# Other shares of filling matmuls in the first attention head, and the lead that they make returned over thirteen heads

## The chip, the cores and the metric

The kernel runs on one core of a Trainium2 chip. The metric is the device time of one execution, in microseconds (us). TensorE is PE in the rows below, its weight load PEld, VectorE is DVE, ScalarE is ACT, GpSimd is POOL and SyncE is SP.

## The reference

One decoder layer over 512 tokens of width 2048: a sparse-attention mixer with 16 heads of 128 in 4 groups, then a SwiGLU feed-forward part, with an RMS norm before each, residual adds and a final norm.

```
proj = h @ w_in                         # q, and three k/v pairs of each group, and gates
s_c = q @ kcc.T + bias_c                # compressed keys (31 blocks)
s_s = q @ k_selected.T + bias           # selected blocks
s_w = q @ kw.T + bias_w                 # window
o = g0 * softmax(s_c) @ vcc + g1 * softmax(s_s) @ v_selected + g2 * softmax(s_w) @ vw
h = h + o @ w_out
h = h + (silu(a) * b) @ ffn_w_out       # a, b = split(rmsnorm(h) @ ffn_w_in)
```

With 512 tokens there are 8 selection blocks and all of them may be taken, so that the selected branch and the window branch both run over all earlier keys. All of it is in float32.

## The kernel before

**Products.** A float32 product is made of three matmuls: each operand is split into a high and a low part, and high x high, low x high and high x low are added up in PSUM (`three`, L343 to L346). For weights the split is made on the way: a raw tile of 128x1024 is loaded (`Weights.load`, L86), ACT copies its high part (`whi`, L102), and DVE subtracts for the low part (`wlo`, L103). There are three raw buffers and four pairs of split ones. A product that needs the next split weights calls `W.take`, and this call writes the splits and loads of the next weights at the same place of the program, two weights ahead. So where a weight is taken decides where `whi` stands in ACT's order, and `wlo` in DVE's. `W.queue` says on which engine's queue the raw loads are issued.

**The attention stage** (L737 to L1024, about 195 to 680 us of the span) has two strands which are written into one program, and each engine runs its part in the order written.

The first strand is the attention of the 16 heads. A head has four tiles of 128 queries, tile t having 128(t+1) keys, and they come in the order 3, 2, 1, 0. `scores` (L885 to L910) makes the scores on PE (`s`), then DVE adds the bias and finds the maximum (`cx` for the compressed keys, two `u` for the other branches, L907) and ACT takes the exponential (L909). The score tile `s` in PSUM exists once, so PE's next scores wait for DVE's reading. `finish` (L912 to L924) scales by sums and gates and transposes 32x32 blocks on DVE (L914 to L922), then stores the probabilities to DRAM on SP's queue (L924). `fetch` (L928) reads them back into `ptr`, and `turn` splits them by the high part on ACT (`pth`, L945) and the low part on DVE (`ptl`, L949): two of 128 columns, two of 256, two of 384, two of 512. `values` multiplies each with the values on PE (`o`), two steps after its `turn`. In the loop over heads (12 steps each) the scores of head h+1 are written into the steps of head h; the text calls what lies between the tile-3 scores of head h and those of head h+1 **stretch h**. In stretch h PE does the scores of head h and the values of head h-1.

The second strand is the filling: `dense()`, the projections of later heads (`qpair`, `kpair`, `vpair`, on PE `proj`), and after those parts of the output projection (`partial`). It is a stream that is cut into units of three matmuls of 512 columns (six of 256), each booked at 650. `yt`, `qh` and `ql` (L396, L369, L370) on DVE and ACT belong to its ends. Four weights make a `qpair`, 32 units.

`pump(h, step)` ends each step. It writes units until the units booked reach a goal: 20800 a head (32 units) up to at = 13, and 22500 a head behind it, with at = h + (step + 4)/12. The first head has no head before it, so its scores stand ahead of the loop, with `pump(-1, min(9 + i, 11.7))` behind each of its tiles, then `pump(0, 1)`, the scores of head 1's tile 3, and `pump(0, 3)`. The raw loads of the whole stage go to POOL's queue (L975), which also issues the bias loads of head 0 and the first two fetches.

Of the kernel before, what the change touches and what calls it, by code (L numbers as in the profile page):

```python
# [43 lines left out]
TP_GAP, HN_GAP = 40, 48  # L44
RESYNC = 14
PT_STEP = 224
SPREAD, N_WARM = UL, 17


# [166 lines left out]
def nsa_block(ctx: ExitStack, tc: tile.TileContext, x, rel_bias, mix_g, ffn_g, fin_g, w_in, w_out,  # L216
              pos_k, w1k, w2k, pos_v, w1v, w2v, f_in, f_out, onehot, out):
    nc = tc.nc
    mm, act, dve, pool = nc.tensor.matmul, nc.scalar.activation, nc.vector, nc.gpsimd
# [12 lines left out]
    W = Weights(nc, rawp, convp, specs)  # L232
# [110 lines left out]
    def three(o, ah, al, bh, bl, start, stop):  # L343
        mm(o, ah, bh, start=start, stop=False, skip_group_check=True)  # L344
        mm(o, ah, bl, start=False, stop=False, skip_group_check=True)  # L345
        mm(o, al, bh, start=False, stop=stop, skip_group_check=True)  # L346

    def ws(ps, gi, g, c0=0, c1=S, start=None, end=None, of=None):

        for u in range(2):  # L350
            cs = slice(128 * u, 128 * (u + 1))
            if end and gi == 3 and u:
                W.ahead(3)
            for k in range(4):
                kk = 4 * gi + k
                st = (kk == 0) if start is None else (start and kk == 0)
                three(ps[u][:, c0:c1], g[0][:, k, cs], g[1][:, k, cs],
                      *(x[:, kk, c0:c1] for x in of or (hn_h, hn_l)), st, kk == KC - 1)
                if end and gi == 3 and k == 3:
                    end(u)  # L360
                yield 650
# [57 lines left out]
    def q_out(ps, h0):  # L419
        def end(u):  # L420
            Q[h0 + u] = tuple(qp.tile([128, S], F32R, name=f"q{n}") for n in "hl")
            split_from(normed(ps[u], SCALE), Q[h0 + u][0], Q[h0 + u][1])

        return end


    with ExitStack() as st1:
# [4 lines left out]
        def proj_tiles(n=2):  # L432
            return [(psx if next(turns) % 4 > 1 else ps1).tile([128, 512], F32, name="proj") for _ in range(n)]
# [5 lines left out]
        with ExitStack() as st0:  # L439
# [121 lines left out]
            ps = proj_tiles()  # L561
# [97 lines left out]
        ps = proj_tiles()  # L659
# [3 lines left out]
        ps = proj_tiles()  # L663
# [7 lines left out]
        ps, hk = proj_tiles(), ps1.tile([128, 256], F32, name="mlp")  # L671
# [8 lines left out]
        ps = proj_tiles()  # L680
# [5 lines left out]
        ps, hv = proj_tiles(4), ps1.tile([128, 256], F32, name="mlp")  # L686
# [30 lines left out]
        ps = proj_tiles()  # L717
        end = q_out(ps, 0)
# [18 lines left out]
    with ExitStack() as st2:  # L737
# [5 lines left out]
        CX = [ap_.tile([128, 32], F32, name=f"cx{t}", bufs=1) for t in range(NT)]  # L743
        PT = ap_.tile([128, 4, PT_STEP * 3 + runs[3]], F32, name="ptr", bufs=1)
        d_p = [dram.tile([4, 32, 4, runs[t]], F32, name=f"d_p{t}") for t in range(NT)]
# [10 lines left out]
        def proj2():  # L756
            pool_ = (psx, ps2)[next(units) % 2]
            return [pool_.tile([128, 512], F32, name="proj") for _ in range(2)]

        def qpair(h0):  # L760
            ps = proj2()
            end = q_out(ps, h0)
            for i in range(4):
                last = ws(ps, i, W.take(), end=end)
                for n, c in enumerate(last):
                    yield c
                    if h0 == H - 2 and i and n in (2, 4, 6):
                        reload_o(3 * i + n // 2 - 4)
                    if h0 == H - 2 and i == 3 and n in (0, 3):
                        split_o(n // 3)  # L770
            done["n"] += 1
            yield None
# [30 lines left out]
        def reload_o(i):  # L803

            nc.sync.dma_start(hn_l[:, i].bitcast(F32), d_o[i // 4][i % 4])

        def split_o(k):
            h, l = (x[:, 2 * k:2 * k + 2] for x in (hn_h, hn_l))
            act(h, l.bitcast(F32), AF.Copy)  # L809
            dve.tensor_tensor(l, l.bitcast(F32), h.bitcast(F32), op=OP.subtract)  # L810
# [40 lines left out]

        def pump(h, step):
            at = h + (step + 4) / STEPS
            goal = 20800 * min(at, 13) + 22500 * max(at - 13, 0)
            while done["ns"] < goal:
                c = next(stream, "end")
                if c == "end":
                    return
                done["ns"] += c or 0
# [15 lines left out]
        def load_bias(h):  # L875
            if h < H:
                TB[h] = ap_.tile([128, S], F32, name="tb")
                (nc.sync if h else pool).dma_start(TB[h], bass.AP(tensor=d_u.tensor, offset=d_u.offset + h * UL + 127,
                                                 ap=[[H * UL - 1, 128], [1, S]]))
# [32 lines left out]
        def finish(h, t):  # L912
            r = HS[h]["sm"][:, t]
            dve.reciprocal(r, r)  # L914
            dve.tensor_mul(r, r, gates[:, t, h])
            for i, p in enumerate(HS[h].pop(t)):
                o = p
                if not i:
                    o = P[t][:, :3, runs[t] - 32:]
                    p = CX[t].unsqueeze(1).to_broadcast([128, 3, 32])  # L920
                dve.tensor_scalar(o, p, r[:, i:i + 1], None, op0=OP.mult)
            dve.transpose(P[t], P[t])  # L922
            for i in range(4):
                nc.sync.dma_start(d_p[t][:, :, i].rearrange("j a r -> a j r"), P[t][32 * i:32 * (i + 1)])  # L924

        def fetch(t, queue=nc.sync):

            queue.dma_start(PT[:, :, PT_STEP * t:PT_STEP * t + runs[t]], d_p[t].rearrange("j a i r -> (j a) i r"))  # L928

        def arrived(rows, c0, t0, step):  # L930
            v = PT[:rows, :, c0:c0 + 32]
            p, i, c = v.ap
            return bass.AP(tensor=v.tensor, offset=v.offset, ap=[p, [step, NT - t0], i, c])

        def turn(h, b, kt):
            n = S - 128 * kt
            th = ap_.tile([128, 512], F32R, name="pth", bufs=3)
            tl = ap_.tile([128, 512], F32R, name="ptl") if b >= 0 else th
            rows = 128 if b >= 0 else 96
            if b < 0:  # L940
                src = arrived(rows, 64, 0, PT_STEP + 64)
            else:
                src = arrived(rows, PT_STEP * kt + 32 * (kt + 1) * b + 32 * kt, kt, PT_STEP + 32 * b)
            th4, tl4 = (x[:rows, :n].rearrange("p (t i s) -> p t i s", i=4, s=32) for x in (th, tl))
            act(th4, src, AF.Copy)  # L945
            if b < 0:
                dve.tensor_tensor(th4[32:64], src[32:64], th4[32:64].bitcast(F32), op=OP.subtract)
            else:
                dve.tensor_tensor(tl4, src, th4.bitcast(F32), op=OP.subtract)  # L949
            HS[h]["t", b, kt] = th[:rows, :n], tl[:rows, :n]  # L950
# [21 lines left out]
                split_from(o, hn_h[:, h], hn_l[:, h])  # L972
            del HS[h]

        W.queue = pool  # L975
        load_bias(0)
        load_bias(1)
        for i in range(4):
            scores(0, 3 - i)
            if i > 1:  # L980
                fetch(5 - i, pool)
            if i:
                finish(0, 4 - i)
            pump(-1, min(9 + i, 11.7))
        finish(0, 0)
        fetch(1)
        fetch(0)
        pump(0, 1)
        scores(1, 3)
        for b in range(2):  # L990
            turn(0, b, 3)
        pump(0, 3)
        for h in range(H):
            seq = [(b, kt) for kt in (3, 2, 1, 0) for b in (0, 1)] + [(-1, 0)]
            for i in range(STEPS):
                if i == 4:
                    load_bias(h + 2)
                if i == 2 and h:
                    fetch(0)
                if i < 9 and (h or i > 1):  # L1000
                    turn(h, *seq[i])
                if i == 8 and h + 1 < H:
                    fetch(3)
                    fetch(2)
                if i == 11 and h + 1 < H:
                    fetch(1)
                if i == 0 and h:
                    finish(h, 0)
                if h + 1 < H:
                    if i == 2:  # L1010
                        drain_to(needed(h + 1))
                    if i % 3 == 2 and h + i > 2:
                        scores(h + 1, 3 - i // 3)
                    elif i % 3 == 0 and i:
                        finish(h + 1, 4 - i // 3)
                if 2 <= i < 10 or i == 11:
                    if i == 2 and h % HPG == 0:
                        drain_to(h)
                    values(h, *seq[min(i - 2, 8)])
                    if i == 11:  # L1020
                        head_out(h)
                pump(h, i)
        W.queue = nc.sync
        drain_to(100)  # L1024
    mixer.close()
# [265 lines left out]
    with tc.tile_pool(name="tmp", bufs=1) as tmp:  # L1291
# [6 lines left out]
        end = plain_out(0, pa)  # L1298
# [4 lines left out]
        for p in range(N_PLAIN):  # L1303
            if p:
                pa = [ps3.tile([128, 512], F32, name="pp") for _ in range(2)]
                end = plain_out(p, pa)
# [430 lines left out]
```

## Time and profile before

| | us |
|---|---|
| median of 3 runs | 2097.61 |
| lowest, highest | 2096.29, 2098.01 |
| the profiled execution | 2096.34 |
| its span | 2094.6 |
| around the span | 1.74 |

Granted clock of TensorE over the span: 0.998. The span runs from the first to the last instruction of the profile. An idle time in brackets behind a row is that of the engine just before this instruction, with what ended it. PE's matmuls overlap: each row of three matmuls of 512 columns starts 0.23 us behind the one before while it shows 0.39 us, so a wait that is short need not show as idle time of PE.

### The profile page before, as it was taken

The page shows a single profiled execution, that of the slowest core. Times are in us where ns is not written, and L with a number is a line of the kernel's source. Part 1 is how long each engine was busy: PE and PEld are TensorE (multiplying, and loading weights), DVE is VectorE, ACT ScalarE, POOL GpSimd, SP SyncE. Part 2 cuts the span into 40 slices and gives each one's busy share as a digit, 9 for nine tenths or more (in the row PEclk, how much of TensorE's full clock was granted, in tenths as well). Part 3 has the DMA queues.
Part 4 walks back from the last instruction along what each step waited for, and adds up shares of the span by engine and source line. Part 5 has one row for each costly group of instructions (what it writes and reads, how often), then busy time and mean ns, then how long its engine had stood idle before and what let it go on. Part 6 is the DMA issues. An engine that isn't in the chain of part 4 may idle for free.

```text
span 2094.6 us, 39078 instructions
## 1 busy us (share of the span) xinstructions
PE 2075.1 (99%) x15236; PEld 1954.1 (93%) x15236; DVE 1627.6 (78%) x2705; ACT 948.6 (45%) x1524; POOL 278.2 (13%) x404
## 2 busy tenths in 40 slices
PE   9999999999999999999999999999999999999998
PEld 7898788898989889899999999999999999999997
DVE  5565777777786457898888888888888688697767
ACT  6344554555455234434434344344343455464445
POOL 2000111111111001022222132221211100000000
PEclk9999999999999999999999999999999999999999
DMA  7555767666677658578878778788755686685667
GB/s 238 171 157 155 198 192 201 189 193 191 204 218 208 240 179 213 151 209 231 216 205 224 205 223 220 196 232 215 199 158 157 208 267 187 194 295 151 196 204 279
DMA packets 321799, 427.68 MB, mean 204 GB/s; under 512 B 40300, under 2 KB 249900, under 8 KB 320973
## 3 DMA queue, kind: packets, MB, share of 16 engines
q1 hardware_dynamic: 261020, 292.18, 43.9%
q0 software_dynamic: 59696, 131.16, 25.8%
q8 instruction: 119, 1.95, 0.4%
q10 hardware_dynamic: 896, 1.84, 0.2%
q14 instruction: 68, 0.55, 0.1%
HBM read 363.12 MB, written 130.13 MB: 235 GB/s over the span
## 4 chain that ended last, share of the span: by engine, by line
PE 67%; DVE 1%; DMA 1%; ACT 0%; issue 0%; SPq 0%; DVEq 0%; ACTq 0%
PE f L344 18%; PE f L345 18%; PE f L346 18%; PE proj L344 2%; PE proj L346 2%; PE proj L345 2%; PE pp L344 1%; PE pp L346 1%; PE pp L345 1%; PE po L346 1%; PE po L344 1%; PE po L345 1%; DMA tlo<-d_w 1%; PE pp L322 0%; DMA tlo<-in_ffn_w_out 0%
## 5 line engine op out<-in xcount | busy, mean ns | idle before, releaser
L103 DVE TENSOR_TENSOR wlo<-raw,whi 128x1024 fp32r<-128x1024 f32 (+2 forms) x223 | 247.5, 1112 | 123.6 <-ACT whi L102 123.0
L102 ACT ACTIVATE whi<-raw 128x1024 fp32r<-128x1024 f32 (+2 forms) x223 | 215.9, 970 | 218.8 <-PE f L346 57.0
L346 PE MATMUL f<-hn_h,wlo 128*128 128x256 f32 x984 | 271.6, 276 | 0.0
L344 PE MATMUL f<-hn_h,whi 128*128 128x256 f32 x984 | 271.6, 276 | 0.0
L345 PE MATMUL f<-hn_l,whi 128*128 128x256 f32 x984 | 271.6, 276 | 0.0
L1229 ACT ACTIVATE whi<-raw 128x1024 fp32r<-128x1024 f32 x123 | 126.2, 1058 | 303.0 <-DVE raw L1125 299.6
L1125 DVE TENSOR_TENSOR tlo<-tt,thi 128x1536 fp32r<-128x1536 f32 (+1 forms) x83 | 145.4, 1752 | 77.8 <-ACT thi L1234 77.3
L344 PE MATMUL proj<-hn_h,whi 128*128 128x512 f32 x504 | 199.9, 397 | 0.0
L346 PE MATMUL proj<-hn_h,wlo 128*128 128x512 f32 x504 | 196.9, 391 | 0.0
L345 PE MATMUL proj<-hn_l,whi 128*128 128x512 f32 x504 | 196.9, 391 | 0.0
L345 PEld LDWEIGHTS f<-hn_l,whi 128*128 128x128 f32 x984 | 184.7, 188 | 0.0
L344 PEld LDWEIGHTS f<-hn_h,whi 128*128 128x128 f32 x984 | 184.7, 188 | 0.0
L346 PEld LDWEIGHTS f<-hn_h,wlo 128*128 128x128 f32 x984 | 184.7, 188 | 0.0
L1234 ACT ACTIVATE thi<-tt 128x1536 fp32r<-128x1536 f32 x82 | 121.9, 1486 | 72.9 <-PE f L345 61.3
L345 PE MATMUL f<-tlo,slot 128*128 128x256 f32 (+1 forms) x546 | 151.7, 278 | 0.0
L344 PE MATMUL f<-thi,slot 128*128 128x256 f32 (+1 forms) x546 | 151.6, 278 | 0.0
L346 PE MATMUL f<-thi,slot 128*128 128x256 f32 (+1 forms) x546 | 151.6, 278 | 0.0
L346 PE MATMUL proj<-whi,hn_l 128*128 128x256 f32 (+2 forms) x496 | 146.1, 295 | 2.9 <-DVE hn_l L810 2.9
L1125 DVE TENSOR_TENSOR wlo<-raw,whi 128x1024 fp32r<-128x1024 f32 x123 | 147.0, 1223 | 1.1 <-ACT whi L1229 1.1
L344 PE MATMUL proj<-whi,hn_h 128*128 128x256 f32 (+2 forms) x496 | 146.6, 295 | 0.8 <-ACT hn_h L809 0.8
L345 PE MATMUL proj<-wlo,hn_h 128*128 128x256 f32 (+2 forms) x496 | 145.6, 294 | 0.0
L345 PE MATMUL f<-wlo,slot 128*128 128x256 f32 (+1 forms) x432 | 121.4, 281 | 0.0
(406 smaller groups left out, 6459.9 us busy)
## 6 DMA issues: line engine op xcount, KB each, us to landing
raw<-in_ffn_w_in SPq DMA_DIRECT2D x135, 512.0 KB, 5.1
d_w<-in_ffn_w_out POOLq DMA_DIRECT2D x80, 512.0 KB, 8.4
rawx<-in_ffn_w_in SPq DMA_DIRECT2D x41, 512.0 KB, 4.8
raw<-in_ffn_w_out SPq DMA_DIRECT2D x73, 256.0 KB, 3.9
tlo<-d_w SPq DMA_DIRECT2D x73, 256.0 KB, 4.3
d_a<-d_a POOLq DMA_DIRECT2D x120, 128.0 KB, 5.7
slot<-d_a SPq DMA_DIRECT2D x18, 768.0 KB, 6.7
raw<-in_nsa_w_in POOLq DMA_DIRECT2D x24, 512.0 KB, 5.0
```

What stands on the lines that cost most here:

```text
L102: self.nc.scalar.activation(hi[:, :n], src, AF.Copy)
L103: self.nc.vector.tensor_tensor(lo[:, :n], src, hi[:, :n].bitcast(F32), op=OP.subtract)
L344: mm(o, ah, bh, start=start, stop=False, skip_group_check=True)
L345: mm(o, ah, bl, start=False, stop=False, skip_group_check=True)
L346: mm(o, al, bh, start=False, stop=stop, skip_group_check=True)
L1125: dve.tensor_tensor(o, a, b, op=OP.subtract)
L1229: act(h, r, AF.Copy)
L1234: act(h, ttf, AF.Copy)
```

## The change

The goal of `pump` gets a lead: 3900 (six units) at the stage's beginning, and less by the same part for each step until it is nothing at at = 13. What the first head writes is no longer a share of this goal, but counts of units: 4, 6, 9 and 11 behind its four tiles, 15 ahead of head 1's tile-3 scores, and 22 behind the first two `turn`s; the first two steps of the loop do not pump. `W.ahead(2)` behind the last tile's scores writes the splits for two weights there, and one `take` has an ahead of one instead of two. The raw loads change to POOL's queue only behind these 22 units.

```diff
+LEAD = 3900
@@ qpair
-                last = ws(ps, i, W.take(), end=end)
+                last = ws(ps, i, W.take(1 if h0 == 2 and i == 1 else 2), end=end)
@@ pump
             at = h + (step + 4) / STEPS
-            goal = 20800 * min(at, 13) + 22500 * max(at - 13, 0)
+            pump_to(20800 * min(at, 13) + 22500 * max(at - 13, 0) + LEAD * max(1 - at / 13, 0))
+
+        def pump_to(goal):
             while done["ns"] < goal:
@@
-        W.queue = pool
         load_bias(0)
         load_bias(1)
         for i in range(4):
@@
             if i:
                 finish(0, 4 - i)
-            pump(-1, min(9 + i, 11.7))
+            if i == 3:
+                W.ahead(2)
+            pump_to(650 * (4, 6, 9, 11)[i])
         finish(0, 0)
         fetch(1)
         fetch(0)
-        pump(0, 1)
+        pump_to(650 * 15)
         scores(1, 3)
         for b in range(2):
             turn(0, b, 3)
-        pump(0, 3)
+        pump_to(650 * 22)
+        W.queue = pool
         for h in range(H):
@@
-                pump(h, i)
+                if h or i > 1:
+                    pump(h, i)
```

On PE the matmuls stay the same, and only the place of units among them changes. Between scores (S with the tile) and values (o with the key tile and the branch) there are, counted in units:

| | before | after |
|---|---|---|
| head 0 | S3 3 S2 3 S1 2 S0 6 | S3 4 S2 2 S1 3 S0 6 |
| stretch 1 | S3 5 o30 o31 o20 3 S2 ... | S3 7 o30 o31 3 o20 3 S2 ... |
| stretch 9, S3 to o01 | 18 | 18 |
| stretch 10, S3 to o01 | 18 | 19 |
| done at S3 of heads 1, 2 | 14, 46 | 15, 51 |
| done at S3 of heads 8, 9, 10 | 238, 270, 302 | 240, 272, 303 |
| done at S3 of heads 11, 12, 13 | 334, 366, 398 | 335, 367, 398 |

Here the heads in the last three lines are those whose tile-3 scores come next. From head 13's tile-3 scores on, the units stand as before.

On SP, in the first head, with d_p the stores of tiles 3, 2, 1, 0 and ptr the fetches; before:

```order
L924 DMA d_p_1880<-p_1871 32x4x160 x4
L924 DMA d_p_1879<-p_1870 32x4x96 x4
L928 DMA ptr<-d_p_1880 128x4x160
L928 DMA ptr<-d_p_1879 128x4x96
L924 DMA d_p_1882<-p_1873 32x4x288 x4
```

and after:

```order
L927 DMA d_p_1880<-p_1871 32x4x160 x4
L87 DMA raw<-in_nsa_w_in 128x4x128 x2
L927 DMA d_p_1879<-p_1870 32x4x96 x4
L931 DMA ptr<-d_p_1880 128x4x160
L931 DMA ptr<-d_p_1879 128x4x96
L87 DMA raw<-in_nsa_w_in 128x4x128 x2
L927 DMA d_p_1882<-p_1873 32x4x288 x4
```

Two raw tiles, in two pieces each, have come over from POOL.

On DVE, in stretch 9, from the last `u` of tile 3 to the tiles of 384 columns; before:

```order
L907 ISA u,mx<-s,tb 128x512
L907 ISA mx 128x1
L949 TENSOR_TENSOR ptl<-ptr,pth 128x256
L914 RECIPROCAL sm<-sm 128x3
L915 TENSOR_TENSOR sm<-sm,gates 128x3
L921 TENSOR_SCALAR p_1873<-cx_1877,sm 128x3x32
L921 TENSOR_SCALAR p_1873<-p_1873,sm 128x4x128 x2
L922 STREAM_TRANSPOSE p_1873<-p_1873 128x1152
L103 TENSOR_TENSOR wlo<-raw,whi 128x1024
L949 TENSOR_TENSOR ptl<-ptr,pth 128x384 x2
```

and after:

```order
L910 ISA u,mx<-s,tb 128x512
L910 ISA mx 128x1
L104 TENSOR_TENSOR wlo<-raw,whi 128x1024
L952 TENSOR_TENSOR ptl<-ptr,pth 128x256
L917 RECIPROCAL sm<-sm 128x3
L918 TENSOR_TENSOR sm<-sm,gates 128x3
L924 TENSOR_SCALAR p_1873<-cx_1877,sm 128x3x32
L924 TENSOR_SCALAR p_1873<-p_1873,sm 128x4x128 x2
L925 STREAM_TRANSPOSE p_1873<-p_1873 128x1152
L952 TENSOR_TENSOR ptl<-ptr,pth 128x384 x2
```

The low part of a weight has moved from behind the transposition to the place right behind the scores; on ACT `whi` has moved likewise, from behind the `pth` of 256 to right behind the exponentials. On DVE, further on in stretch 9, from the first `ptl` of 512 columns on; before:

```order
L949 TENSOR_TENSOR ptl<-ptr,pth 128x512
L914 RECIPROCAL sm<-sm 128x3
L915 TENSOR_TENSOR sm<-sm,gates 128x3
L921 TENSOR_SCALAR p_1872<-cx_1876,sm 128x3x32
L921 TENSOR_SCALAR p_1872<-p_1872,sm 128x4x96 x2
L922 STREAM_TRANSPOSE p_1872<-p_1872 128x896
L103 TENSOR_TENSOR wlo<-raw,whi 128x1024
L949 TENSOR_TENSOR ptl<-ptr,pth 128x512
L396 SCALAR_TENSOR_TENSOR yt<-proj,ybc 128x512
L370 TENSOR_TENSOR ql<-yt,qh 128x512
L103 TENSOR_TENSOR wlo<-raw,whi 128x1024
```

and after:

```order
L104 TENSOR_TENSOR wlo<-raw,whi 128x1024
L952 TENSOR_TENSOR ptl<-ptr,pth 128x512
L917 RECIPROCAL sm<-sm 128x3
L918 TENSOR_TENSOR sm<-sm,gates 128x3
L924 TENSOR_SCALAR p_1872<-cx_1876,sm 128x3x32
L924 TENSOR_SCALAR p_1872<-p_1872,sm 128x4x96 x2
L925 STREAM_TRANSPOSE p_1872<-p_1872 128x896
L397 SCALAR_TENSOR_TENSOR yt<-proj,ybc 128x512
L371 TENSOR_TENSOR ql<-yt,qh 128x512
L104 TENSOR_TENSOR wlo<-raw,whi 128x1024
L952 TENSOR_TENSOR ptl<-ptr,pth 128x512
```

Both low parts and one `yt` with its `ql` now stand ahead of the second `ptl` of 512, where one low part did.

From the tile-3 scores of a stretch to its second `ptl` of 512, DVE's order holds, more than before: in stretch 1 a low part and two pairs of `yt` and `ql`; in 2 and 3 two such pairs; in 4 two `v0l` (a value projection's end in place of `yt` and `ql`); in 5 to 7 one pair; in 8 a low part and two `v0l`; in 9 and 10 a low part and one pair; in 11 one pair; in 12 and 13 nothing. In 2 to 7 the first low part stands between the two `ptl` of 384; in 8 to 13 the first two stand right behind the scores of tiles 3 and 2, as shown. What has come ahead of the second `ptl` of 512 is missing behind it.

## Rows read from the trace of the kernel before

**Rows 1.** The page: span, and busy time of each engine over it.

```profile
span 2094.6 us, 39078 instructions
PE 2075.1 (99%) x15236; PEld 1954.1 (93%) x15236; DVE 1627.6 (78%) x2705; ACT 948.6 (45%) x1524; POOL 278.2 (13%) x404
```

**Rows 2.** Waits of PE, 195 to 580 us: total, times, longest.

```profile
PE o L344 <- ACT pth L945: 1.7, 1, 1.7
PE s L344 <- DVE mx L907: 1.6, 2, 0.9
PE o L344 <- issue: 0.6, 1, 0.6
```

**Rows 3.** Timeline of PE, head 0: start, duration, operation, idle before and releaser.

```profile
201.31 0.39 PE L344 MATMUL proj<-hn_h,whi 128*128 128x512 f32 x1
...
202.00 0.40 PE L344 MATMUL proj<-hn_h,whi 128*128 128x512 f32 x1
...
204.41 0.40 PE L344 MATMUL s<-k0h,qh 128*128 128x288 f32 x1 [0.88 <-DVE mx L907]
...
210.73 0.40 PE L344 MATMUL s<-k0h,qh 128*128 128x288 f32 x1 [0.77 <-DVE mx L907]
...
220.98 0.30 PE L344 MATMUL o<-pth,v0h 128*128 128x128 f32 x1 [0.62 <-issue]
...
223.70 0.38 PE L344 MATMUL o<-pth,v0h 128*128 128x256 f32 x1 [1.66 <-ACT pth L945]
```

**Rows 4.** DMA issues, 190 to 235 us: xcount, KB each, us to landing.

```profile
raw<-in_nsa_w_in SPq DMA_DIRECT2D x4, 256.0 KB, 3.0
raw<-in_nsa_w_in POOLq DMA_DIRECT2D x4, 256.0 KB, 4.7
```

**Rows 5.** Timeline of ACT: the first parts of 256 columns, stretch 1.

```profile
223.23 0.72 ACT L945 ACTIVATE pth<-ptr 128x256 fp32r<-128x256 f32 x2 [1.20 <-DMA ptr<-d_p]
```

**Rows 6.** A head's busy time: us, PE, PEld, DVE, ACT, POOL, clock, DMA share, GB/s.

```profile
460.00:490.00 30.00, 30.00 (x147) 24.95 (x146) 23.60 (x67) 15.12 (x40) 4.47 (x6) 1.00 0.69 192
```

**Rows 7.** Waits of DVE and ACT, 460 to 490 us: total, times, longest.

```profile
ACT cx L909 <- DVE mx L907: 10.5, 4, 3.7
DVE ptl L949 <- ACT pth L945: 4.2, 3, 1.5
...
DVE ql L370 <- ACT qh L369: 1.4, 2, 0.7
```

**Rows 8.** Timeline of DVE, stretch 9, and the next stretch's first row.

```profile
460.54 0.18 DVE L907 CUSTOM_DVE_ANT_0 cx<-s,biasc 128x31 f32<-128x31 f32 x1
...
463.24 0.43 DVE L949 TENSOR_TENSOR ptl<-ptr,pth 128x256 fp32r<-128x256 f32 x1 [1.28 <-ACT pth L945]
...
475.12 0.68 DVE L949 TENSOR_TENSOR ptl<-ptr,pth 128x512 fp32r<-128x512 f32 x1
...
477.10 0.69 DVE L370 TENSOR_TENSOR ql<-yt,qh 128x512 fp32r<-128x512 f32 x1 [0.70 <-ACT qh L369]
...
478.05 1.23 DVE L103 TENSOR_TENSOR wlo<-raw,whi 128x1024 fp32r<-128x1024 f32 x1 [0.26 <-ACT whi L102]
...
490.44 0.18 DVE L907 CUSTOM_DVE_ANT_0 cx<-s,biasc 128x31 f32<-128x31 f32 x1
```

**Rows 9.** Timeline of PE: stretch 9's first and last tile-3 scores, its o01, stretch 13's beginning.

```profile
457.16 0.29 PE L344 MATMUL s<-k0h,qh 128*128 128x288 f32 x1
...
458.46 0.28 PE L346 MATMUL s<-k0h,ql 128*128 128x256 f32 x1
...
476.23 0.39 PE L345 MATMUL o<-ptl,v0h 128*128 128x512 f32 x1
...
576.85 0.29 PE L344 MATMUL s<-k1h,qh 128*128 128x288 f32 x1
```

**Rows 10.** Timeline of DVE, stretch 14, where a low part stands right behind the scores.

```profile
617.52 0.18 DVE L907 CUSTOM_DVE_ANT_0 cx<-s,biasc 128x31 f32<-128x31 f32 x1
...
620.86 1.22 DVE L103 TENSOR_TENSOR wlo<-raw,whi 128x1024 fp32r<-128x1024 f32 x1 [1.93 <-ACT whi L102]
```

## The prediction, made before the changed kernel was timed

> **What bounds the kernel now.** I read the page first. PE is busy 2075.1 of 2094.6 us [rows 1], so a change of order can gain only some of the 19.5 us that are left, or lose by making PE wait. The change touches the attention stage alone, so next I read what PE waits for there, from the first scores to head 13: three lines, 1.7 + 1.6 + 0.6 = 3.9 us, five waits [rows 2]. The timeline puts all of that into 20 us of head 0 [rows 3]: 0.88 and 0.77 ahead of the scores of tiles 2 and 0, which wait until DVE has read the ones before them, then 0.62 and 1.66 ahead of the first values of 128 and of 256 columns. Idle time understates a wait, since matmuls overlap. From start to start, against the pitch usual for the same shape, these four stand at 1.04, 0.94, 0.78 and 1.83, and the matmuls behind the last two at 0.17 and 0.35: **5.1 us**. That is all that the first head can give.
>
> Behind head 0 the stage looks calm: PE is busy 30.00 of 30.00, DVE 23.60, ACT 15.12 [rows 6]. But I asked what DVE and ACT do in the rest of their time. DVE's waits are for ACT (`ptl` for `pth` 4.2, `ql` for `qh` 1.4), ACT's longest is for DVE (10.5) [rows 7]: in this stretch DVE waits for neither PE nor a transfer. They run as a loop of their own, and its period, from `cx` at 460.54 to `cx` at 490.44, is 29.90 [rows 8]. PE's tile-3 scores start at 457.16 in stretch 9 and at 576.85 in stretch 13 [rows 9], 29.92 a head. A head's 32 units at 0.69 (202.00 less 201.31 [rows 3]) are 22.1, and its scores and values are 7.6 by the pitch of their shapes: 29.7, so some 0.25 a head is already waits, about 1.5 us from head 7 on. The two loops go at the same pace, and the slack between them is small: DVE's second `ptl` of 512 columns starts at 475.12 and takes 0.68, so it is ready at 475.80, and PE uses it at 476.23 [rows 8, 9]. **0.43 us is what DVE may be later there.**
>
> **Part 1: head 0's shares.** By the last score tile 9 units instead of 8 are in place, and between the values of 128 and of 256 columns stand three where there was none. One unit of 0.69 comes into waits on DVE that PE would sit through: of 1.04 + 0.94, 1.3 stays. The 2 units more ahead of the first values (1.4) cover 0.78 and 0.17, and the three behind them (2.1) the 1.83 and 0.35. Gain 0.69 + 3.13 = **3.8 us**; by idle times alone 0.69 + 0.62 + 1.66 = 3.0 (low end); 5.1 is the most.
>
> **Part 2: the queue.** Four issues of 256 KB go from POOL to SP, where the same shape lands in 3.0 instead of 4.7 [rows 4]. Behind them on SP wait the stores of tile 0 and, for the second pair, head 1's first stores. The first pair runs beside the fetch on which `pth` of 256 waited 1.20 [rows 5], and takes transfer time from it. No row shows this meeting. Its cost is from 0 (ACT's wait is met by the three new units) to 1.7, the difference of the two landing times, taken as a measure of what a transfer loses to its neighbours there; no gain, as no split waits for these loads. I take 0, nearest to what the cover gives, and keep 1.7 for the range.
>
> **Part 3: the lead and its return.** Units are moved, not added. But a unit that comes earlier takes its weight earlier, and `whi` and `wlo` move up in ACT's and DVE's order past `pth` and `ptl`, which PE needs at a fixed place. I count X, from `cx` to the end of the second `ptl` of 512. Before, X = 475.80 - 460.54 = 15.26 [rows 8].
>
> In stretches 9 and 10 three things are added. A low part right behind the scores waits for its `whi`, which waits for the exponentials: 1.93 [rows 10] where `ptl` waited 1.28 [rows 8], +0.65. The same again in tile 2: +0.5. Ahead of the second `ptl` of 512 stand one more low part (1.18 at the spacing of its kind; the row with a wait shows 1.23), `yt` and `ql` (0.68 and 0.69), `ql`'s wait of 0.70 and the low part's 0.26, less what overlaps: +3.4 [rows 8]. X = 15.3 + 0.65 + 0.5 + 3.4 = 19.8, taken as 20.0.
>
> PE asks for it 476.23 - 458.74 = 17.5 after its tile-3 scores end (the last starts at 458.46 and takes 0.28 [rows 9]), with 18 units between; with 19 it is 18.2. So the wait is D + X - 17.5 or - 18.2, where D is how far `cx` starts behind the end of the scores (1.80 in stretch 9 before). PE's waits shorten D again, down to nearly 0 (I take 0.14). In stretch 9, D = 0.25 gives **2.75**; DVE's order then takes longer than PE's, D grows to 1.3, and stretch 10 gives **3.0**. Stretch 11, with one pair more (X about 18.7), gives 1.25; stretch 8, with a low part and two `v0l`, 0.5; stretch 12 has X as before, 0. Sum 7.5.
>
> Stretch 1 has the most on DVE ahead of both `ptl` of 512 (a low part, two pairs): 1.2 for the first and 2.2 for the second, 3.4. Stretches 2 and 3, with two pairs, X = 18.7 and PE 18 or 19 units behind: 0.7 and 1.35, 2.0. Stretches 4 to 6: 0, stretch 7: 0.7. Stretch 13, where PE is at its known waits and two low parts come earlier, +1.5.
>
> **Sum.** Waits before: 5.1 + 1.5 = 6.6. After, to stretch 12: 1.3 (head 0) + 3.4 + 2.0 + 0.7 + 7.5 = 14.9. With stretch 13's 1.5 that is +9.8. Nothing behind takes it back, for from head 13's scores on the units stand as before and PE is the bound. The profiled execution took 2096.34 us, 1.74 more than its span; 2096.3 + 9.8 = **2106 us**. It lies 1.3 under the median of 2097.6 and at the lowest of the three runs, so against the median the same sum would read 2107.4.
>
> The least by this reckoning is D at its floor of 0.14 everywhere: 2.65 + 1.9 + 1.0 for stretches 9 to 11, 2.5 in stretches 1 to 3, 1.3 in head 0 and nothing else, 9.4 against 6.6 with up to 1.5 for stretch 13: +3 to +5, so 2099 to 2101. The most is the sum with part 2's 1.7 and part 1's low end (+0.8): 2108.5.
>
> **A rule against this.** DVE's 23.60 and ACT's 15.12 of 30.00 [rows 6] leave room on both. The Trainium skill (Perfetto Trace Analysis, Identifying the Most-Contended Engine) calls occupancy a fair measure for Vector and Scalar and says to optimise the engine with the highest first; by it neither of the two limits anything here, and filling PE's gaps pays in full; the time that this gives is the first rival's, below. The rows of waits speak against it: two half-idle engines that wait for each other have a period of 29.90 [rows 7, 8].
>
> **The rivals.**
>
> *The loop has room, and the change pays (faster).* With `wlo` and `yt` moved, DVE works while it waited for `pth` before; up to 4.2 + 1.4 = 5.6 of a head [rows 7] could be filled, and the order of stretches 2 to 6, which puts the low part between two `ptl` of 384, shortens the loop. Then DVE comes ahead of PE by a microsecond a head, D is at its floor when stretch 9 begins, and what is late there is made up. Price: part 1's 3.8, with up to 1.5 of the small waits: 2091 to 2092.5. Against it: PE's use of the second `ptl` of 512 is at 17.5 or 18.2 whatever D is, and X stands at 20. It decides if X is below 18 in stretches 9 to 11, that is if the added 4.6 is under 2.7.
>
> *Gain and loss cancel (same).* Part 1's 3.8 comes, and the late stretches cost half of what I reckon: D at its floor, and X about 19. 3.8 + 1.5 gained against 3.4 + 2 or so: 2096 to 2101.
>
> *Slower, by the first stretch's fetch rather than the order.* The raw loads on SP keep back head 0's fetch, PE waits there up to 1.7, and the rest cancels: 2098.
>
> **How the numbers follow.** A difference of 0.2%, 4.2 us, is about what a measurement of this kernel can tell from no change, so faster is under 2093.4 and slower over 2101.8. Slower by DVE's order has 0.65, most of it from 2102 to 2109, with likeliest 2106. The two cases inside the bound have 0.24 together, 2095 to 2101.8, and the gain 0.11. The range, 2095 to 2110, takes in the first two, with 1.5 above the most for a loop whose lag grows on; what is left out is the gain and a little more loss.
>
> **What would show it.** PE's waits in head 0 on `pth` are gone, and the ones on `mx` are near 1.3: part 1. New waits of PE on `ptl` (values of 512 columns) in stretches 1 to 3 and, longest, 9 and 10, some 3 us each; DVE's period from `cx` to `cx` there at 32 to 33, not 29.9: part 3. Tile-3 scores of head 13 at 585 instead of 576.85. I am wrong if they start at or before 577, if PE waits for no `ptl` in stretches 9 to 11, or if the second `ptl` of 512 ends less than 18 us behind `cx` there; and wrong on the queue if `pth` of 256 in stretch 1 waits over 2 us for its fetch and PE with it.

## Result: slower by twice what was forecast

The changed kernel takes 2115.83 us (median of 5 runs, 2114.91 to 2117.60), the kernel before 2096.43 (5 runs): a ratio of 1.0092, interval 1.0077 to 1.0107, or 19.4 us. The forecast was 2106.0, with 2095 to 2110: right in its sign and in where the loss sits, outside its range in size. The profiled execution took 2116.36 us, with a span of 2114.6.

The page of the changed kernel, against [rows 1]: PE's busy time grew by only 7 us, the span by 20.

```profile
span 2114.6 us, 39085 instructions
PE 2082.2 (98%) x15236; PEld 1955.8 (92%) x15236; DVE 1629.6 (77%) x2705; ACT 948.4 (45%) x1524; POOL 275.4 (13%) x400
```

PE's waits from 195 to 600 us (total, times, longest), against [rows 2]. The one wait for `pth` of 1.7 has become seven, and ten for `ptl` are new:

```profile
PE o L345 <- ACT pth L948: 7.6, 7, 2.3
PE o L346 <- DVE ptl L952: 6.1, 10, 0.9
PE s L345 <- DVE mx L910: 1.2, 3, 0.5
```

That is 14.9 us of idle time where [rows 2] add up to 3.9; 0.9 of it lies in stretch 13, which begins at 593.03, so 14.0 stands ahead of it. More than half is PE's wait for ACT's `pth`. Tile-3 scores of head 13 start at 593.03 instead of 576.85 [rows 9], 16.2 later. From head 15's scores to the last 30 us of the kernel the distance stays between 18.7 and 18.8 us, so nearly all of the loss was made in the attention stage and nothing gives it back. The last 30 us add another 1.2, to the 20.0 between the two spans.

To place it, I took each matmul's distance to the next, less the usual distance for its shape, and added these up by stretch, split into those ahead of which PE idled and those that were slow without an idle time. The measured columns are differences to the kernel before, row by row; the forecast's rows for 2 to 12 are waits as they would be afterwards, with those of before taken off in a line of their own, and its other rows are differences too:

| | forecast | measured | of it waits | of it slow matmuls |
|---|---|---|---|---|
| head 0 | -0.7 | -0.7 | -1.0 | +0.3 |
| stretch 1 | +0.3 | 0.0 | +0.4 | -0.4 |
| 2 and 3 | +2.0 | +2.6 | +2.4 | +0.2 |
| 4 to 7 | +0.7 | +0.9 | +0.8 | +0.1 |
| 8 | +0.5 | +1.85 | +1.7 | +0.1 |
| 9 | +2.75 | +5.05 | +3.5 | +1.6 |
| 10 | +3.0 | +4.15 | +2.7 | +1.5 |
| 11 | +1.25 | +1.7 | +1.6 | +0.1 |
| 12 | 0.0 | +0.7 | +0.7 | +0.1 |
| waits of before in 7 to 12 | -1.5 | off in each row | | |
| 13 | +1.5 | +1.6 | +1.1 | +0.5 |
| 14 to the end | 0.0 | +2.1 | | |

Stretches 8 to 12 hold 13.5 of the 20.0 us between the two spans, where 6.0 was forecast.

DVE in stretch 9, against [rows 8]: the low parts stand where the order put them, and the first waits 1.93 for its `whi`, as in [rows 10].

```profile
465.45 0.18 DVE L910 CUSTOM_DVE_ANT_0 cx<-s,biasc 128x31 f32<-128x31 f32 x1
...
468.79 1.22 DVE L104 TENSOR_TENSOR wlo<-raw,whi 128x1024 fp32r<-128x1024 f32 x1 [1.93 <-ACT whi L103]
...
477.39 1.23 DVE L104 TENSOR_TENSOR wlo<-raw,whi 128x1024 fp32r<-128x1024 f32 x1 [1.85 <-ACT whi L103]
...
483.85 1.23 DVE L104 TENSOR_TENSOR wlo<-raw,whi 128x1024 fp32r<-128x1024 f32 x1 [0.25 <-ACT whi L103]
484.99 0.68 DVE L952 TENSOR_TENSOR ptl<-ptr,pth 128x512 fp32r<-128x512 f32 x1
```

From `cx` to the end of the second `ptl` of 512 it is 485.67 - 465.45 = 20.2 us (X, before 15.26). PE's rows there, against 476.23 in [rows 9], which had no idle time:

```profile
484.39 0.50 PE L345 MATMUL o<-pth,v0h 128*128 128x512 f32 x1 [2.26 <-ACT pth L948]
485.73 0.49 PE L346 MATMUL o<-ptl,v0h 128*128 128x512 f32 x1 [0.84 <-DVE ptl L952]
...
487.92 0.63 PE L346 MATMUL proj<-hn_l,whi 128*128 128x512 f32 x1
...
490.17 0.39 PE L346 MATMUL proj<-hn_l,whi 128*128 128x512 f32 x1
```

PE waits first for ACT's `pth`, which stands behind `qh` and `whi` on ACT, then for the `ptl` made from it. ACT itself was free: its `qh` waited 4.36 for DVE's `yt`.

```profile
482.24 0.63 ACT L370 ACTIVATE qh<-yt 128x512 fp32r<-128x512 f32 x1 [4.36 <-DVE yt L397]
482.77 1.04 ACT L103 ACTIVATE whi<-raw 128x1024 fp32r<-128x1024 f32 x1
483.72 0.61 ACT L948 ACTIVATE pth<-ptr 128x512 fp32r<-128x512 f32 x1
```

Among ACT's waits from 430 to 580 there is none of a `whi` for its raw load, so the loads, which moved with the splits, were not late. Behind PE's waits, a unit's matmuls take 0.63 instead of 0.39. The windows say why (us, busy time of PE, PEld, DVE, ACT, POOL, granted clock, DMA share, GB/s):

```profile
484.00:486.00 2.00, 0.77 (x2) 0.46 (x3) 2.00 (x3) 0.33 (x1) 0.52 (x1) 1.00 0.27 66
486.00:488.00 2.00, 2.00 (x7) 1.53 (x7) 1.27 (x3) 1.15 (x2) 0.22 (x1) 0.59 0.52 127
488.00:490.00 2.00, 2.00 (x7) 1.56 (x6) 1.26 (x7) 1.36 (x6) 0.00 (x0) 0.55 0.45 155
490.00:492.00 2.00, 2.00 (x11) 1.64 (x10) 1.79 (x6) 0.08 (x1) 0.00 (x0) 1.00 0.95 311
```

The granted clock falls to between 0.5 and 0.6 behind the two waits, that is mostly 1.2 GHz, and is back at 2.4 by 490. Such a fall is in the trace of before too, behind a wait of 2.15 us at 607.86 (stretch 13, the same columns), and I had read that place without making a price of it:

```profile
606.00:608.00 2.00, 0.14 (x1) 0.14 (x2) 2.00 (x3) 0.00 (x0) 0.00 (x0) 1.00 1.08 352
608.00:610.00 2.00, 2.00 (x10) 2.00 (x11) 1.47 (x7) 0.92 (x5) 0.00 (x0) 0.54 0.98 257
```

### The profile page after: what moved, and what is told of

The parts are those of the page before. It is cut to its first block, busy times and chain, and to the rows that moved or that the text cites. A ratio compares the mean times of both kernels' runs of the same rounds, so it can differ in the third digit from the quotient of the medians.

```text
span 2114.6 us, 39085 instructions
## 1 busy us (share of the span) xinstructions
PE 2082.2 (98%) x15236; PEld 1955.8 (92%) x15236; DVE 1629.6 (77%) x2705; ACT 948.4 (45%) x1524; POOL 275.4 (13%) x400
## 4 chain that ended last, share of the span: by engine, by line
PE 68%; DVE 1%; DMA 0%; ACT 0%; issue 0%; DVEq 0%; ACTq 0%
PE f L346 19%; PE f L345 19%; PE f L347 19%; PE proj L345 2%; PE proj L346 2%; PE proj L347 2%; PE pp L347 1%; PE pp L346 1%; PE pp L345 1%; PE po L346 1%; PE po L347 1%; PE po L345 1%; PE pp L323 0%; DMA tlo<-in_ffn_w_out 0%; DVE slot L1134 0%; PE o L346 0%
```

## The experiments

The theory after this reading: the loss is DVE's (and ACT's) order around the second `ptl` of 512, and a share of it the clock. The rivals: head 0's shares or the queue; units that stand in other places on PE; a loss that grows with the lead. Four kernels first, on one chip, where the kernel before took 2099.85 us (16 runs).

**No lead.** LEAD = 0; head 0's shares and the queue change stay.

```diff
-LEAD = 3900
+LEAD = 0
```

> The changed kernel with a lead of 0: head 0 keeps its new shares and the queue change, stretch 1 has 31 units instead of 36, and from stretch 2 on DVE's and PE's order is that of before. If the loss comes from the lead's order of DVE in the later stretches (theory), all of it goes: tile-3 scores of head 13 within 2 us of 576.85, waits of PE on ptl in stretches 2 to 12 as before, and a time of 2093 to 2097 us, since head 0 gives 0.7 to 3 us. If head 0's shares or the queue cause the loss (rival), it stays over 2105 us.

Measured: 2099.18 us (11 runs), ratio 0.9994 (0.9985 to 1.0003). Head 13's scores start at 577.60, and DVE's X is 15.3 in stretches 2 to 12 (15.6 in 10). So neither head 0's shares nor the queue costs anything that can be measured, and the whole loss hangs on the lead. The expected 2093 to 2097 were counted from 2096.4, so from 3.4 less to 0.6 more than before; measured are 0.7 less, inside the noise. The shares alone gain nothing that can be told: head 0 gives its 0.7, and then PE runs into the values of 256 columns without the three units ahead of them.

```profile
224.18 0.39 PE L345 MATMUL o<-pth,v0h 128*128 128x256 f32 x1 [2.02 <-ACT pth L948]
```

The clock is 0.67 and 0.50 in the four microseconds from 224, and stretch 1 is 0.8 us worse than before: 0.4 less in waits, 1.3 more in slow matmuls.

**Splits one step later.** What a `take` asks for is written behind the next step's `turn` and `finish` in the loop's heads 7 to 12; PE's order stays.

```diff
     def ahead(self, n):
+        self.want = max(self.want, self.nt + n)
+        if not self.hold:
+            self.flush()
+
+    def flush(self):
         last = len(self.specs)
-        while self.ncv < min(self.nt + n, last):
+        while self.ncv < min(self.want, last):
@@
+                W.flush()
+                W.hold = 7 <= h < 13
                 if h or i > 1:
                     pump(h, i)
+                W.hold = False
```

> The changed kernel, but in the loop's heads 7 to 12 the splits and loads that a take asks for are written one step later, behind the next step's turn and finish. PE's order of matmuls stays that of the changed kernel; on ACT and DVE the low parts of stretches 8 to 12 stand again where they stood before, and only one yt with its ql (or two v0l) still stands ahead of the second ptl of 512. Theory (DVE's order makes PE wait): X in stretches 9 and 10 falls from 20.2 to about 17.3, PE waits there under 1 us each, the clock stays at 1.00 there, and 9 to 11 of the 13.5 us lost in stretches 8 to 12 come back: 2103 to 2108 us. Rival (the places of the units on PE themselves cost it, or the lead as such): 2113 to 2117 us.

Measured: 2106.57 us (5 runs), ratio 1.0032 (1.0019 to 1.0045). PE's waits from 425 to 555 us, first here and then in the changed kernel (425 to 570):

```profile
PE o L351 <- DVE ptl L957: 0.9, 3, 0.3
PE s L350 <- DVE mx L915: 0.2, 1, 0.2
```

```profile
PE o L345 <- ACT pth L948: 5.3, 4, 2.3
PE o L346 <- DVE ptl L952: 2.8, 4, 0.8
```

X is 17.3 in stretches 9 and 10, no clock falls there, and 11.5 of the 13.5 us of stretches 8 to 12 are back. PE's matmuls stand exactly as in the changed kernel, so their places cost at most the 2 us that are left; the `yt` and `ql` that still stand ahead of the `ptl` can account for these, which is not shown by itself. Over the whole stage 9.6 us came back and not 11.5, because stretches 13 and 14, where the held splits end, took some 1.2 more and stretch 1 varied by 0.5.

**Raw loads on POOL again**, all else changed.

```diff
+        W.queue = pool
         load_bias(0)
@@
         pump_to(650 * 22)
-        W.queue = pool
```

> The changed kernel with only the queue undone: raw loads on POOL from before head 0, as before. Theory (the queue is worth nothing): within 1.5 us of the changed kernel's 2115.8. Rival (the raw loads on SP hold back head 0's fetch, up to 1.7 us): 2114 or less, with pth of 256 in stretch 1 waiting less than 1.0.

Measured: 2117.13 us (4 runs), ratio 1.0079 (1.0066 to 1.0093), inside the changed kernel's own interval. The queue is worth nothing that can be measured. In the changed kernel `pth` of 256 waits 1.02 for its fetch in stretch 1, not the 1.20 of [rows 5], and with the loads on POOL it waits 1.27; the feared meeting of the loads and the fetch does not show.

**Doses of DVE time** in the kernel before, to measure PE's wait and the clock by themselves.

```diff
                 dve.tensor_tensor(tl4, src, th4.bitcast(F32), op=OP.subtract)
+                if b == 1 and kt == 0:
+                    for _ in range({3: 2, 5: 4, 7: 6, 9: 8}.get(h, 0)):
+                        dve.tensor_tensor(tl4, src, th4.bitcast(F32), op=OP.subtract)
```

> The kernel before, with the last subtraction of the second ptl of 512 columns repeated 2, 4, 6 and 8 times more in stretches 4, 6, 8 and 10 (0.61 us each: 1.2, 2.4, 3.7, 4.9 us of DVE, the result is the same). Nothing else is moved. Both theories expect PE to wait 0.8, 2.0, 3.2 and 4.5 us for it, a slack of 0.43 less, 10.5 together. Theory A (a longer wait also lowers TensorE's clock, as the trace of the changed kernel shows in stretches 9 and 10): behind the two or three longer ones the granted clock falls to between 0.5 and 0.7 for some 4 us, at 1.6 us each: 2110 to 2113 us. Theory B (the slow matmuls in stretches 9 and 10 have another cause): clock 1.00 all through, 2106 to 2108 us.

Measured: 2116.12 us (4 runs), ratio 1.0073 (1.0058 to 1.0088). The expected times were counted from 2096.4; against the kernel before on the same chip it is 16.3 us more, where theory A had 14 to 17 and theory B 10 to 12. In the traces 1.3 us more stand in stretch 1, ahead of the first dose (below). PE's rows behind the four doses:

```profile
328.79 0.50 PE L345 MATMUL o<-ptl,v0h 128*128 128x512 f32 x1 [0.29 <-DVE ptl L952]
...
391.93 0.50 PE L345 MATMUL o<-ptl,v1h 128*128 128x512 f32 x1 [2.37 <-DVE ptl L952]
...
456.81 0.80 PE L345 MATMUL o<-ptl,v1h 128*128 128x512 f32 x1 [3.69 <-DVE ptl L952]
...
523.62 0.50 PE L345 MATMUL o<-ptl,v0h 128*128 128x512 f32 x1 [4.41 <-DVE ptl L952]
```

10.8 us of idle time where 10.5 was expected, but that the sums meet is partly luck: a dose took 0.73 and not 0.61 (X is 21.1 with eight of them), and D differs from stretch to stretch. With the D and X of this trace, the prediction's D + X - 17.5 gives 0.4, 2.7, 4.4 and 4.4 us, so the way from DVE's lateness to PE's wait is right. And the windows behind the second, third and fourth:

```profile
392.00:394.00 2.00, 2.00 (x9) 1.67 (x10) 1.17 (x2) 1.49 (x2) 0.00 (x0) 1.00 0.11 31
...
458.00:460.00 2.00, 2.00 (x7) 1.52 (x6) 1.51 (x3) 1.13 (x2) 0.00 (x0) 0.50 0.00 0
460.00:462.00 2.00, 2.00 (x6) 1.61 (x5) 1.47 (x7) 1.16 (x5) 1.50 (x2) 0.50 0.18 20
...
524.00:526.00 2.00, 2.00 (x7) 1.58 (x6) 1.04 (x3) 1.80 (x3) 0.00 (x0) 0.55 0.00 0
526.00:528.00 2.00, 2.00 (x7) 1.59 (x6) 1.94 (x5) 0.29 (x1) 0.56 (x1) 0.59 0.00 0
```

Nothing else had been moved, so the waits themselves bring the fall. Its price was some 3 us behind 3.69 and 1.7 behind 4.41, and nothing behind 2.37: it is not a fixed sum, and the length of a wait alone does not tell whether it comes.

That shows best in stretch 1, where this kernel is still the kernel before. The wait ahead of the values of 256 columns was 1.66 in the trace of before [rows 3], and the clock stayed up; here it was 1.53, and the clock fell. First the window of before, then row and window of this run:

```profile
224.00:226.00 2.00, 1.92 (x10) 1.58 (x10) 1.88 (x8) 0.00 (x0) 1.26 (x2) 1.00 0.61 160
```

```profile
223.70 0.48 PE L344 MATMUL o<-pth,v0h 128*128 128x256 f32 x1 [1.53 <-ACT pth L945]
...
224.00:226.00 2.00, 2.00 (x6) 1.59 (x6) 1.92 (x7) 0.00 (x0) 1.39 (x2) 0.50 0.75 177
```

In the same way the waits of 1.34 and 0.30 in stretch 1 of the changed kernel (239.83 and 240.63) left the clock at 1.00, and those of 1.35 and 0.30 in the kernel with the loads on POOL brought it to 0.52. So a fall of some 1.3 to 2 us comes and goes in stretch 1 without any change in PE's order.

**A lead that is kept: two, three, four, five units.** If the place of the takes in a step sets DVE's order, the loss should not grow with the lead, but go up and down. These four keep one lead to at = 12.9, so that PE's order in stretches 2 to 12 is that of before, to the unit, and only the phase of the takes differs.

```diff
-LEAD = 3900
+LEAD = 1300        # 1950, 2600, 3250
@@
-            pump_to(... + LEAD * max(1 - at / 13, 0))
+            pump_to(... + (LEAD if at < 12.9 else 0))
```

> The changed kernel with a lead of two units that isn't given back step by step but kept until at = 12.9. PE's order in stretches 2 to 12 is then that of before, to the unit; on DVE the order of stretches 8 to 10 of the changed kernel (a low part right behind the scores of tiles 3 and 2, and a third one with yt and ql ahead of the second ptl of 512) stands in every stretch from 2 to 12. Theory (the loss is DVE's order, set by where in a step the takes fall): each of the 11 stretches loses 3 to 4.5 us, waits and clock together, as 9 and 10 did in the changed kernel: 2128 to 2148 us. Rival (the loss grows with the lead, or comes from units standing in other places on PE): with a third of the lead and PE's order of before, 2096 to 2102 us.

> As the kernel with a lead of two units, with three. On DVE no low part stands right behind the scores; ahead of the second ptl of 512 stand one yt with its ql (or two v0l) more than before, as in stretch 7 of the changed kernel, which lost 0.86 us. Theory: X near 17.6, 0.5 to 1 us in each of 11 stretches, clock 1.00: 2101 to 2108 us. Rival (loss grows with the lead): more than with a lead of two.

> As the kernel with a lead of two units, with four. DVE's order in stretches 2 to 12 is that of stretches 5 and 6 of the changed kernel, which lost nothing. Theory: nothing is lost in stretches 2 to 12, head 0 gives 0.7 to 1, and stretch 13, where the lead ends, is unknown within 3 us: 2093 to 2099 us. Rival (loss grows with the lead): the slowest of the three.

> As the kernels with a kept lead of two, three and four units, with five. DVE's order in stretches 2 to 12 is that of stretches 2 to 4 of the changed kernel: two pairs of yt and ql ahead of the second ptl of 512 (lost 1.1 and 1.5 there), or two v0l (lost nothing). Theory: 8 stretches at 1.1 to 1.5 and 3 at about 0, less head 0's gain: 6 to 11 us more than before, clock 1.00. Rival (four units or more are enough, the loss of shorter leads being one of too little lead): as with four.

The kernel before took 2098.62 us beside the first three (15 runs) and 2098.70 beside the fourth (21 runs). X and the period from `cx` to `cx` are those of stretch 10, and D is how far `cx` starts behind the end of the scores:

| lead | time | ratio (interval) | D | X | period |
|---|---|---|---|---|---|
| none (before) | | | 1.66 | 15.3 | 29.9 |
| 2 units | 2155.95 | 1.0270 (1.0254 to 1.0285) | 0.61 | 20.1 | 34.5 |
| 3 units | 2109.41 | 1.0049 (1.0035 to 1.0063) | 0.72 | 17.8 | 31.0 |
| 4 units | 2095.58 | 0.9988 (0.9979 to 0.9996) | 0.61 | 15.9 | 29.7 |
| 5 units | 2113.54 | 1.0072 (1.0058 to 1.0086) | 0.61 | 18.4 | 31.5 |

A lead of two units costs 57 us, one of four gains: a loss that grows with the lead is out, and so are the places of the units on PE, which are the same in all four in stretches 2 to 12. The smallest lead puts the order of stretches 8 to 10 of the changed kernel into all eleven stretches, and each costs about what stretches 9 and 10 cost there. PE's waits from 195 to 640 us with two units, and with four (the second run of it, below):

```profile
PE o L345 <- ACT pth L948: 22.9, 13, 2.1
PE o L346 <- DVE ptl L952: 10.1, 12, 0.8
```

```profile
PE o L346 <- DVE ptl L952: 5.5, 5, 3.1
PE s L345 <- DVE mx L910: 0.7, 2, 0.5
PE o L345 <- ACT pth L948: 0.6, 2, 0.5
```

DVE's `cx` of stretches 9 and 10 and the second `ptl` of 512 of the latter, with two units:

```profile
499.06 0.18 DVE L910 CUSTOM_DVE_ANT_0 cx<-s,biasc 128x31 f32<-128x31 f32 x1
...
518.38 0.68 DVE L952 TENSOR_TENSOR ptl<-ptr,pth 128x512 fp32r<-128x512 f32 x1
...
533.70 0.18 DVE L910 CUSTOM_DVE_ANT_0 cx<-s,biasc 128x31 f32<-128x31 f32 x1
```

and with four:

```profile
460.61 0.19 DVE L910 CUSTOM_DVE_ANT_0 cx<-s,biasc 128x31 f32<-128x31 f32 x1
...
475.82 0.68 DVE L952 TENSOR_TENSOR ptl<-ptr,pth 128x512 fp32r<-128x512 f32 x1
...
490.22 0.18 DVE L910 CUSTOM_DVE_ANT_0 cx<-s,biasc 128x31 f32<-128x31 f32 x1
```

In these rows it is stretch 9: 518.38 + 0.68 - 499.06 = 20.0 against 475.82 + 0.68 - 460.61 = 15.9, and a period of 34.6 against 29.6. With X = 15.9 and D = 0.61 the `ptl` is ready 16.5 behind the scores, a microsecond before PE's 17.5, and the loop takes PE's own 29.7. Two units cost 57.3 us more than before where 32 to 52 was expected: the eleven stretches cost 4.9 us more than before on average, 3.1 in waits and 1.8 in slow matmuls, and stretch 1, which the expectation left out, adds 4.5. Three units cost 10.8 (5 to 12 expected), five 14.8 (6 to 11 expected): there the stretches with two pairs cost 1.3 to 1.8 each, and stretch 1 adds 1.5, with a fall of the clock in it.

**Four units again, and ended earlier** (at = 12.4 in place of 12.9).

> The kernel with a kept lead of four units once more, for its interval. Theory: head 0 and stretch 1 give 3 us, stretches 4, 8 and 12 (with two v0l ahead of the second ptl of 512) cost 1 together: 2 to 4 us less than before, a ratio of 0.9980 to 0.9992. Rival (the first comparison was chance): 0.9995 or more.

> The kernel with a kept lead of four units, with the lead taken back at at = 12.4 instead of 12.9, so that stretch 13 has DVE's order of before and not two splits of reloaded heads and a low part ahead of its second ptl of 512, for which PE waits 3.1 us in the kernel with the lead to 12.9. Theory: stretch 13 costs 7.3 as before instead of 7.9, up to 2 less if the clock doesn't fall: 0.3 to 2 us less than the kernel with the lead to 12.9. Rival (the units missing behind stretch 12's values make PE wait elsewhere): 1 to 3 us more.

Measured: 2096.20 us, ratio 0.9990 (0.9981 to 0.9998), and 2095.86, ratio 0.9987 (0.9978 to 0.9996), 11 runs each against 21 of before. Both beat before and the changed kernel; the gain of 2 to 3 us is at the edge of what can be told, but three comparisons agree, two of which share the same runs of before. In the traces, head 0 and stretch 1 together stand at 3.0 us over the pitch with four units where they stood at 5.9 before: **this is part 1's gain, 2.9 us**, against 3.0 to 3.8 as reckoned. Stretches 4, 8 and 12, with their two `v0l`, still make PE wait 0.3 to 0.7 for `ptl`, where the first expectation let nothing be lost. The two ends differ by nothing that can be measured: the earlier one trades the `ptl` wait of 3.1 in stretch 13 for the `hn_l` waits of before.

**Splits of the reloaded heads on POOL**, in the kernel before. Stretch 13 holds 7.3 us over the pitch, more than head 0, so it looked like the place to gain.

```diff
             act(h, l.bitcast(F32), AF.Copy)
-            dve.tensor_tensor(l, l.bitcast(F32), h.bitcast(F32), op=OP.subtract)
+            pool.tensor_tensor(l, l.bitcast(F32), h.bitcast(F32), op=OP.subtract)
```

> The kernel before with the six subtractions of the reloaded heads (hn_l, line 810) on POOL instead of DVE. It bears on where this stage can still gain: stretch 13 holds 7.3 us of waits and slow matmuls, more than head 0's 5.1. If DVE's load there is the cause (theory), 7.2 us less on DVE in stretches 13 and 14 brings 3 to 6 us: 2091 to 2094 us. Rival: POOL is slower than DVE at it, and PE waits for POOL instead: 2096 to 2105 us.

Measured: 2106.50 us (4 runs), ratio 1.0038 (1.0023 to 1.0052); the rival holds. POOL's operation, and PE's longest new wait (195 to 640 us):

```profile
L810 POOL TENSOR_TENSOR hn_l<-hn_l,hn_h x6: 2341/2362/2418, 599.7 to 624.2; 128x1024 fp32r<-128x1024 f32 x6
```

```profile
PE proj L346 <- POOL hn_l L810: 5.0, 4, 1.6
```

2.36 us each where DVE takes 1.2 (1.18 to 1.23 for the same six in the trace of before), and PE waits for them.

## Why the prediction was right in sign and short in size

**Part 1** holds: 0.7 in the scores as reckoned, the value waits of head 0 gone from the trace, 2.9 us where a lead follows that does no harm.

**Part 2** holds: nothing that can be measured. The 1.7 kept for the range was not needed.

**Part 3** holds in its mechanism, and X was right where it was worked out from rows: 20.0 reckoned for stretches 9 and 10, 20.2 and 20.1 measured; 18.7 for stretch 11, 18.4 measured; the waits stand ahead of the second tile of 512 columns, in the stretches that were named. One sign was drawn too narrowly: the waits were to be on `ptl`, and more than half of the idle time is on the `pth` from which it is made (2.26 of 3.10 in stretch 9), because the late `yt` on DVE holds back ACT's order too. What failed are terms of the sum:

1. **The clock had no term.** Behind the waits of stretches 9 and 10 PE ran at about half its rate for some 4 us: +3.1 us, put at nothing. The price could have been read from stretch 13 of before, where a wait of 2.15 is followed by a clock of 0.54 (above) and some 1.7 us of slow matmuls.
2. **D's floor.** I took 0.14; measured, `cx` never starts less than 0.61 behind the end that the profile shows for the scores. That alone is about 0.5 in stretches 2, 3 and 11 and 0.6 in stretch 9 (D 0.85 instead of 0.25). In stretch 10 D was to grow to 1.3 and fell back to 0.61, so the waits there were 2.7 where 3.0 was forecast: PE's wait takes the lag away again.
3. **Stretches 8 and 12.** I gave stretch 8's low part and two `v0l` a wait of 0.5, with no working shown; X was 19.7 and the loss 1.85. The `v0l` wait for their `v0h` on ACT, and the low part behind them for its `whi`:

```profile
449.10 0.44 DVE L404 SCALAR_TENSOR_TENSOR v0l<-proj,ymul,v0h 128x256 fp32r<-128x256 f32 x1
450.08 0.48 DVE L404 SCALAR_TENSOR_TENSOR v0l<-proj,ymul,v0h 128x256 fp32r<-128x256 f32 x1 [0.54 <-ACT v0h L403]
451.03 1.23 DVE L104 TENSOR_TENSOR wlo<-raw,whi 128x1024 fp32r<-128x1024 f32 x1 [0.46 <-ACT whi L103]
```

From the first `v0l` to the low part's start it is 1.93, of which 1.0 is waiting. Stretch 12 was to have X as before and lose nothing; X was 16.6, and PE waited 0.53 for DVE ahead of the tile-0 scores.

4. **The credit of 1.5** for waits already there in stretches 7 to 12 was about right and hides part of the miss. In the trace of before, the first scores of tile 0 start 0.2 to 0.3 late in stretches 7, 9, 10 and 11 without an idle time that shows, and a value in stretch 8 as much; in the changed kernel these are gone. In stretch 9 of before it is 0.38 from a unit's last matmul to the scores, where 0.23 is usual:

```profile
480.58 0.39 PE L346 MATMUL proj<-hn_h,wlo 128*128 128x512 f32 x1
480.96 0.40 PE L344 MATMUL s<-k0h,qh 128*128 128x288 f32 x1
```

The measured column has them taken off in each row, so stretches 8 to 12 stand at some 15 us of waits and slow matmuls where 7.5 was forecast.

5. **Behind stretch 13** I let nothing be lost; 2 us were. One is in stretch 14, which starts with DVE later behind PE (`cx` 4.35 behind the first scores instead of 3.34), and 1.2 in the last 30 us of the kernel, of which no run here shows the cause. Nor do all units stand as before from head 13's scores on: twice in stretch 13 there are 3 and 2 units between two values where there were 2 and 3.

The sum of idle times came out near by chance: 14.9 forecast to stretch 12, 14.0 in the view of waits. But 6.6 was taken off for before where the same view shows 3.9, and a wait costs more than its idle time. That is counted from the end shown for a matmul, 0.16 behind the point where the next one usually starts (0.39 against 0.23), the first matmul behind a wait hands on some 0.1 later, and the clock may fall.

**The rivals.** That the loop has room was to be decided by X below 18 in stretches 9 to 11; it was 18.4 to 20.2, so it fell for this change. As a mechanism it is real: with a lead of four X is 15.9 and the change pays. Occupancy, the ground for it, does not tell these cases apart: over stretches 2 to 12 DVE is busy for 261 us with two units and for 257 with four, ACT for 170 and 169, and 60 us lie between the two kernels. That gain and loss cancel needed X about 19 and stretches 9 to 11 at 2 us or so; they cost 10.9. The transfer rival fell with the queue.

What stays open: why waits of the same length, at the same place of the same order, bring the clock down in one execution and not in another, and why 2.37 us left it alone.

## To carry to other kernels

When filling work is moved, don't stop at the engine that it fills: list what each moved unit pulls along on the other engines, and count for every consumer how long the feeding engine now takes from its fixed start (here X) against the time at which it is asked for. Here the order depended on the phase and not on the amount, so try neighbouring amounts (two, three, four, five units) before judging a schedule. A wait of TensorE of 1.3 us or more, alone or with a second one right behind it, should be priced with a fall of the clock, 1.3 to 3 us here, and as a range that begins at nothing, since it does not always come.

## What the runs showed of the hardware

Waits of PE are followed by a fall of the granted clock in some cases and not in others. It fell behind waits of 1.53, 2.02, 2.15, 3.69 and 4.41 us, and behind 1.35 with 0.30 and 1.39 with 0.84 shortly after: the lowest window of 2 us behind each of them stands at 0.50 to 0.55. It stayed at 1.00 behind waits of 1.66 and 2.37 us and behind 1.34 with 0.30. The price was 1.3 to 3 us in slow matmuls. In the kernel with a lead of two it came in each of stretches 1 to 12, and in stretches 2 to 12 PE lost some 20 us in slow matmuls beside 34 us in waits.

A low part of 128x1024 takes 1.2 us on DVE and 2.36 us on POOL, at least while the other engines run beside it.
